# A two-layer diffusion transformer on one core: the background modulation units distributed anew over three stretches

## The chip, the cores and the metric

The kernel runs on one core of one Trainium2 chip. The metric is device time in microseconds from one launch, the median of three runs. A core has a tensor engine (PE; its weight loads are listed as PEld), a vector engine (DVE), a scalar engine (ACT), a general-purpose engine (POOL) and a sync engine (SP), which here only issues DMAs. Each engine works through its own queue in order and waits on semaphores for the others.

## The reference, cut to what matters

512 tokens of a sequence and 256 of a context, width 2048, go through two layers. Both layers modulate their normalised input and gate their output with vectors that come from one matrix each and two conditioning vectors (`c` for the sequence, `c_ctx` for the context):

```python
sc, scc = jax.nn.silu(c), jax.nn.silu(c_ctx)
for i in range(2):
    shift, scale, gate = jnp.split((sc @ ada_w[i] + ada_b[i])[:, None, :], 3, axis=-1)
    shift_c, scale_c, gate_c = jnp.split(scc @ ada_w[i] + ada_b[i], 3, axis=-1)
    h = rmsnorm(x, norm_w[i]) * (1.0 + scale) + shift
    hc = rmsnorm(xc, norm_w[i]) * (1.0 + scale_c) + shift_c
    y, yc = even_mix(h, hc, ...) if i == 0 else odd_mix(h, hc, ...)
    x = x + gate * y
    if i == 0:
        xc = xc + gate_c * yc
return rmsnorm(x, final_norm)
```

`even_mix` is an in-projection, a pooling branch, latent attention over 12 heads and an out-projection; `odd_mix` is an in-projection, a matrix memory (four heads, with gates), a window attention and an out-projection. In layer 1 the context only feeds keys, values and the initial state, so its gate is not needed.

## The kernel before, in words

All matrix products are done in three parts (high by high, high by low, low by high), so every weight block of [128, 512] is loaded by SP into `wraw` (3 buffers, `load_w`, L114), cast to its high part by ACT (L108, `wh`) and subtracted into its low part by DVE (L109, `wl`; 4 buffers each, that is two loads). `tmode` (L289 for the sequence's 512 columns, L291 for the context's 256) and `kmode` (L302) issue the products.

**The modulation** is a [2048, 6144] matrix by two vectors for each layer, cut into 24 units of 512 columns. Units 0 to 7 are layer 0's shift and scale, 8 to 11 its gate, 12 to 19 layer 1's shift and scale, 20 to 23 its gate. Units 0 to 7 are done on PE at the start. The others are background work (`Background`, `ada_vec_steps`), handed out in steps by calls of `bg.step(n)` between other work. A step takes one chunk of 128 rows: SP loads `at` (256 KB, L160, 4 buffers), DVE multiplies and adds it into `acc0` (L164), and where the context needs it too (units below 20) ACT multiplies `at` in place by the context's factor (L167) and POOL adds that into `acc1` (L169). After 16 chunks one step for each accumulator transposes and reduces it on DVE (L174, L175), and some steps into the next unit a tiny product (`pb`, L181) and four DVE additions (L131) finish the unit. So a unit has 18 steps, or 17 from unit 20 on, which touch neither ACT nor POOL.

**Stretch A, layer 0's in-projection.** `in_group(g)` does one group of 256 columns: four quarters, each with one `load_w`, a `bg.step(2)`, the products of four chunks with sequence and context, and another `bg.step(2)`, that is 16 steps for a group. There are twelve: two for the latent queries, four for the pooling branch (the second and fourth with `pool_mean` and `pool_mix` between their quarters: L512 to L528 on DVE, ACT and POOL, and the products `ppx` of L545 on PE), six for the attention's gates. Units 8 to 17 lie here: 180 steps in at most 192.

**Stretch B, layer 0's out-projection.** `out0(g, vs)` does a group of 256 columns in four quarters with a `bg.step(4)` in each: groups 1 to 5 with sequence and context, 6 and 7 with the sequence alone, then 0, 6 and 7 with the context alone, while `hx_chunks` prepares layer 1's rows on DVE, ACT and POOL. `out0_evac` (L855 to L864) evacuates a group with work on DVE, ACT and POOL. Units 18 to 23 lie here (18 and 19 with the context, 20 to 23 without): 104 steps in at most 160. `h_chunk` needs units 12 to 19; the gate of layer 1 is first read in the last out-projection.

**Stretch C, layer 1's in-projection**, has no background work before. In it `mv_group(h)` makes the values of heads 1 to 3 of the matrix memory (four quarters, `kmode`), after the gates of all heads were worked out in a long chain of small DVE and PE operations (pool `gs`, closed by `eg.close()`, its last reader among the buffers L1148). Then one group of keys and values of the window attention (weights `odw[5]`).

The order of instructions on PE is written out by hand only inside `manual_schedule`; elsewhere a scheduler orders each engine's queue, SP's too, by the order of the program and its own estimate of when an instruction's inputs and buffers are there. The pools of a stack reuse each other's space: a tile in a reused place waits until the earlier tile's last reader is done.

## Time and profile before

| | |
|---|---|
| median of three runs | 2376.73 us (2375.67 to 2378.95) |
| profiled execution, first to last instruction | 2376.1 us |
| PE busy | 2269.3 us (96%) |
| DVE busy | 1492.2 us (63%) |
| ACT busy | 1041.0 us (44%) |
| POOL busy | 462.4 us (19%) |
| mean granted clock of PE | 0.988 of 2.4 GHz |

The profile is of one execution. Times in its rows are microseconds from the span's start. A row of windows gives the busy time of each engine in a stretch, with the number of instructions that touch it, then the granted clock as a share of full speed. A row of a group gives line, engine, operation, what is written from what, the count, then busy time in us and mean ns of one, and after the last bar the engine's idle time just before and what ended it. A row of waits gives who waited for whom, total us, times and the longest.

### The profile page before, as it was taken

To read this page: it belongs to the slowest core of one execution; us is meant where nothing else is said; L and a number is where in the kernel's file an instruction comes from. 1 tells how busy PE (TensorE), PEld (TensorE's weight loads), DVE (VectorE), ACT (ScalarE), POOL (GpSimd) and SP (SyncE) were. 2 spreads that over 40 slices of the span, in tenths; PEclk is the share of its full clock that TensorE was granted. 3 is DMA by queue.
4 is the path that set the end of the run, shared out by engine and by line. 5 is a ranking of instruction groups with operands and counts; after the bars stand their busy time and mean duration, and the time that the engine had idled before them with its cause. 6 is when DMAs were issued, how large, how long until landed. Compare 5 with 4: busy or idle time off the path is not lost.

```text
span 2376.1 us, 34745 instructions
## 1 busy us (share of the span) xinstructions
PE 2269.3 (96%) x12920; PEld 1897.2 (80%) x12920; DVE 1492.2 (63%) x2748; ACT 1041.0 (44%) x2054; POOL 462.4 (19%) x393
## 2 busy tenths in 40 slices
PE   5999998899999999999999999999999999998997
PEld 3678887788888888878888798998888877776886
DVE  5578888866466666668767822522555576778435
ACT  4234444443344444454224522222555556666333
POOL 0015575754100000016311200000000000003111
PEclk9999999999999999999999999999999999999998
DMA  9854454553211111255675322123222211113333
GB/s 384 312 195 160 169 186 155 186 200 137 81 47 58 47 52 54 70 169 206 227 246 190 136 100 80 56 79 112 98 97 96 102 58 65 60 63 116 133 120 138
DMA packets 118586, 311.27 MB, mean 131 GB/s; under 512 B 13676, under 2 KB 21356, under 8 KB 118416
## 3 DMA queue, kind: packets, MB, share of 16 engines
q1 hardware_dynamic: 111536, 281.73, 34.5%
q0 software_dynamic: 6880, 27.32, 3.0%
q8 instruction: 101, 1.65, 0.3%
q14 instruction: 69, 0.57, 0.1%
HBM read 279.37 MB, written 29.62 MB: 130 GB/s over the span
## 4 chain that ended last, share of the span: by engine, by line
PE 70%; DVE 8%; issue 3%; ACT 2%; DMA 2%; POOL 2%; SPq 0%; DVEq 0%; ACTq 0%; POOLq 0%
PE px L289 20%; PE px L302 11%; PE pj L619 6%; PE pc L291 5%; PE px L1419 5%; PE s L683 5%; PE pc L302 3%; PE om L726 3%; PE pj L639 2%; PE s L1419 2%; PE po L1338 2%; PE tp L708 2%; POOL acc L169 1%; DVE wl L109 1%; DMA at<-in_ada_dram 1%
## 5 line engine op out<-in xcount | busy, mean ns | idle before, releaser
L109 DVE TENSOR_TENSOR wl<-wraw,wh 128x512 fp32r<-128x512 f32 (+2 forms) x556 | 429.9, 780 | 422.9 <-ACT wh L108 414.8
L108 ACT CAST wh<-wraw 128x512 fp32r<-128x512 f32 (+2 forms) x556 | 324.4, 589 | 605.8 <-PE pc L291 137.3
L169 POOL TENSOR_TENSOR acc<-acc,at 128x512 f32<-128x512 f32 x180 | 285.1, 1584 | 282.6 <-ACT at L167 272.5
L164 DVE SCALAR_TENSOR_TENSOR acc<-at,st,acc 128x512 f32<-128x512 f32 x240 | 246.5, 1027 | 53.5 <-DMA at<-in_ada_dram 49.6
L167 ACT ACTIVATE at<-at,st 128x512 f32<-128x512 f32 x180 | 130.0, 724 | 180.8 <-DVE acc L164 157.2
L302 PE MATMUL px<-wh,hxh 128*128 128x512 f32 (+2 forms) x512 | 174.2, 340 | 0.2 <-ACT akx L1201 0.2
L302 PE MATMUL px<-wl,hxh 128*128 128x512 f32 (+2 forms) x512 | 173.7, 339 | 0.0
L302 PE MATMUL px<-wh,hxl 128*128 128x512 f32 (+2 forms) x512 | 173.6, 339 | 0.0
L289 PE MATMUL px<-h0h,wl 128*128 128x512 f32 x384 | 155.6, 405 | 10.4 <-DVE wl L109 10.3
L289 PE MATMUL px<-h0h,wh 128*128 128x512 f32 x384 | 155.9, 406 | 1.3 <-ACT wh L108 1.3
L289 PE MATMUL px<-h0l,wh 128*128 128x512 f32 x384 | 154.1, 401 | 0.0
L291 PE MATMUL pc<-h0l,wh 128*128 128x256 f32 x400 | 113.8, 285 | 0.0
L291 PE MATMUL pc<-h0h,wh 128*128 128x256 f32 x400 | 113.7, 284 | 0.0
L291 PE MATMUL pc<-h0h,wl 128*128 128x256 f32 x400 | 113.7, 284 | 0.0
L302 PEld LDWEIGHTS px<-wh,hxh 128*128 128x128 f32 x512 | 96.2, 188 | 12.9 <-ACT sz L1262 1.0
L302 PEld LDWEIGHTS px<-wl,hxh 128*128 128x128 f32 x512 | 96.2, 188 | 11.3
L302 PEld LDWEIGHTS px<-wh,hxl 128*128 128x128 f32 x512 | 96.2, 188 | 11.0
L289 PEld LDWEIGHTS px<-h0h,wl 128*128 128x128 f32 x384 | 73.5, 191 | 31.1 <-DVE wl L109 13.9
L289 PE MATMUL px<-zxh,wh 128*128 128x512 f32 x224 | 89.6, 400 | 2.5 <-DVE x L855 2.5
L289 PE MATMUL px<-zxh,wl 128*128 128x512 f32 x224 | 89.2, 398 | 2.5 <-DVE wl L109 2.4
L289 PEld LDWEIGHTS px<-h0h,wh 128*128 128x128 f32 x384 | 73.6, 192 | 20.1 <-ACT wh L108 2.6
L289 PE MATMUL px<-zxl,wh 128*128 128x512 f32 x224 | 89.6, 400 | 0.0
(875 smaller groups left out, 6209.9 us busy)
## 6 DMA issues: line engine op xcount, KB each, us to landing
at<-in_ada_dram SPq DMA_DIRECT2D x256, 256.0 KB, 2.9
at<-in_ada_dram SPq DMA_DIRECT2D x64, 512.0 KB, 8.0
wraw<-in_od_in_dram SPq DMA_DIRECT2D x64, 512.0 KB, 3.4
wraw<-in_ev_in_dram SPq DMA_DIRECT2D x56, 512.0 KB, 4.2
wraw<-in_ev_out_dram SPq DMA_DIRECT2D x44, 512.0 KB, 4.2
wraw<-in_od_out_dram SPq DMA_DIRECT2D x36, 512.0 KB, 3.4
wraw<-in_od_oz_dram SPq DMA_DIRECT2D x32, 512.0 KB, 3.4
xt<-in_xT_dram SPq DMA_DIRECT2D x16, 384.0 KB, 7.5
```

The source lines that it names most:

```text
L108: S.copy(h, src)
L109: low.tensor_tensor(l, src, h, op=ALU.subtract)
L164: V.scalar_tensor_tensor(acc[0], at, st[:, kc, 0:1], acc[0], op0=ALU.mult, op1=ALU.add)
L167: S.mul(m, at, st[:, kc, 1:2])
L169: G.tensor_tensor(acc[1], acc[1], m, op=ALU.add)
L289: T.matmul(px[b], w_, Hx[kc][r_], start=s0, stop=s1)
L291: T.matmul(pc[b], w_, Hc[kc][r_], start=s0 and b == 0, stop=s1, skip_group_check=True)
L302: T.matmul(p_, h_, w_, start=s0, stop=s1, skip_group_check=True)
L619: T.matmul(t, w_, r_[:, sl], start=kc == 0 and n == 0, stop=kc == 3 and n == 2)
L683: T.matmul(s[:, c0 - k0 : c1 - k0], l_, r_[:, c0:c1], start=n == 0, stop=n == 4)
L726: T.matmul(o[:, :256], v_[:, 6 - nk + b, :], p_[:, b, :], start=b == 0 and n == 0, stop=b == nk - 1 and n == 2)
L1419: T.matmul(px[b], w_, Hs[kc][r_], start=first and i == 0 and n == 0, stop=last and i == len(kcs) - 1 and n == 2)
```

## The change

The units are handed out differently. Units 8 to 13 (108 steps) stay under the in-projection, with 16 steps for a group of the latent queries, 4 for the first group of each pooling pair and none for the second, 12 for the first four gate groups and 16 for the last two: 120 in all. Units 14 to 19 (108 steps) go under the out-projection with its 16 steps for a group, and are finished before the sequence's rows of layer 1 are begun, that is within groups 1 to 7 (112 steps). Units 20 to 23 (68 steps) go under layer 1's values, 20 steps for a group of `mv_group` (60) and 16 under the keys and values of the window attention, with buffers of their own (pool `ada1`, opened just after `gs` is closed). The instructions of a unit are the same as before. The diff also takes out comments and docstrings, which leaves every line at its number up to the insertions.

```diff
-    bg = Background(range(8, 18), pp, ap_, 4, "ta", 6)
-
-    def in_group(g, between=()):
+    bg = Background(range(8, 14), pp, ap_, 4, "ta", 6)
+
+    def in_group(g, between=(), steps=(1, 1)):
         px, pc = new_px(2), new_pc()
         for kq in range(4):
             w = load_w(win[g, kq])
-            bg.step(2)
+            bg.step(steps[0])
             tmode(px, [pc[:, b, :] for b in range(2)], w, range(4 * kq, 4 * kq + 4), HX0, HC0, kq == 0, kq == 3)
-            bg.step(2)
+            bg.step(steps[1])
             if kq < len(between):
                 between[kq]()
...
-        px, pc = in_group(2 + g)
+        px, pc = in_group(2 + g, steps=(2, 2))
...
-        px, pc = in_group(4 + 2 * pr)
+        px, pc = in_group(4 + 2 * pr, steps=(1, 0))
...
-        qx, qc = in_group(5 + 2 * pr, (lambda: mean(1), lambda: mix(0), lambda: None, lambda: mix(1)))
+        qx, qc = in_group(5 + 2 * pr, (lambda: mean(1), lambda: mix(0), lambda: None, lambda: mix(1)), (0, 0))
...
-        px, pc = in_group(8 + i)
+        px, pc = in_group(8 + i, steps=(2, 1) if i < 4 else (2, 2))
...
-    bg = Background(range(18, 24), pp, tz, 4, "ht", 3)
+    bg = Background(range(14, 20), pp, tz, 4, "ht", 3)
...
     for g in (6, 7):
         out0(g, (0,))
-    # layer 1's rows of the sequence, while the context goes through
+    bg.finish()
+
     ezx.close()
...
     for _ in hxs:
         pass
-    bg.finish()
     etz.close()
...
     eg.close()
 
-    # v of the other heads
+
+    ea = ExitStack()
+    bg = Background(range(20, 24), pp, opool(ea, "ada1"), 4, "atr", 1)
+
+
     def mv_group(h):
         px, pc = new_px(2), new_pc()
         pv = [px[b // 2][:, 256 * (b % 2) : 256 * (b % 2) + 256] for b in range(4)]
         for kq in range(4):
             w = load_w(odw[1 + h, kq])
+            bg.step(5)
...
         w = load_w(odw[5, kq])
+        bg.step(4)
         tmode(px, [pc[:, b, :] for b in range(2)], w, range(4 * kq, 4 * kq + 4), HX, HC, kq == 0, kq == 3)
+    bg.finish()
+    ea.close()
```

## Rows read from the trace of the kernel before

**Rows 1.** The page: busy time, share of the span and instructions of each engine.

```profile
PE 2269.3 (96%) x12920; PEld 1897.2 (80%) x12920; DVE 1492.2 (63%) x2748; ACT 1041.0 (44%) x2054; POOL 462.4 (19%) x393
```

**Rows 2.** Windows: latent queries, pooling, gate groups 1 and 2, 3 and 4, 5 and 6.

```profile
core 0: us, PE busy (x) PEld busy (x) DVE busy (x) ACT busy (x) POOL busy (x), PEclk, DMA share, GB/s
164.95:239.27 74.32, 71.54 (x400) 61.75 (x399) 66.25 (x72) 33.09 (x52) 43.10 (x30) 0.98 0.49 167
239.27:401.34 162.07, 149.41 (x812) 127.69 (x811) 140.26 (x161) 74.32 (x123) 94.35 (x70) 0.96 0.49 168
401.34:482.61 81.27, 73.70 (x391) 61.53 (x389) 69.76 (x70) 38.16 (x63) 61.34 (x42) 0.96 0.55 188
482.61:552.43 69.82, 68.97 (x390) 59.03 (x389) 38.15 (x47) 26.32 (x45) 28.42 (x21) 1.00 0.49 166
552.43:619.74 67.31, 67.31 (x389) 58.75 (x388) 38.41 (x52) 23.32 (x41) 25.90 (x19) 1.00 0.36 122
```

**Rows 3.** Waits: total us, times, longest; SP of 164:625, PE of 239:401 and 401:483.

```profile
SPq L160 <- POOL acc L169: 232.8, 143, 4.3
...
PE ppx L545 <- ACT wpoolh L108: 4.9, 2, 4.3
PE cps L247 <- DVE ssqc L454: 2.4, 1, 2.4
...
PE px L289 <- DVE wl L109: 6.3, 7, 1.9
```

**Rows 4.** The chain that ended last, gate groups 1 and 2, shares by line.

```profile
by line: issue 21.7%; DMA at<-in_ada_dram 19.4%; POOL acc L169 16.7%; DVE acc L164 14.1%; DVE wl L109 10.5%; ACT at L167 10.4%; DVE atr L174 3.0%; ACT wh L108 2.6%; DVE red L175 1.8%; DVE acc L162 0.7%; ACTq L167 0.3%; POOLq L169 0.1%; DVEq
```

**Rows 5.** Windows of the pooling stretch, lines L545, then L247 alone; columns PE, PEld.

```profile
239.27:401.34 162.07, 6.13 (x24) 4.58 (x24) 0.96 0.49 168
...
239.27:401.34 162.07, 1.50 (x12) 1.41 (x12) 0.96 0.49 168
```

**Rows 6.** Groups by line in 401:483, 1102:1136, 1204:1238 and 1238:1284.

```profile
L164 DVE SCALAR_TENSOR_TENSOR acc<-at,st,acc 128x512 f32<-128x512 f32 x37 | 41.7, 1127 | 8.7 <-DMA at<-in_ada_dram 8.1
L109 DVE TENSOR_TENSOR wl<-wraw,wh 128x512 fp32r<-128x512 f32 x15 | 22.4, 1498 | 4.1 <-ACT wh L108 4.0
...
L169 POOL TENSOR_TENSOR acc<-acc,at 128x512 f32<-128x512 f32 x12 | 19.6, 1635 | 6.3 <-ACT at L167 5.6
L164 DVE SCALAR_TENSOR_TENSOR acc<-at,st,acc 128x512 f32<-128x512 f32 x14 | 14.6, 1043 | 3.0 <-DMA at<-in_ada_dram 2.8
L174 DVE STREAM_TRANSPOSE atr<-acc 128x512 f32<-128x512 f32 x2 | 1.3, 686 | 0.0
...
L164 DVE SCALAR_TENSOR_TENSOR acc<-at,st,acc 128x512 f32<-128x512 f32 x15 | 11.6, 775 | 4.7 <-DMA at<-in_ada_dram 4.4
L109 DVE TENSOR_TENSOR wl<-wraw,wh 128x512 fp32r<-128x512 f32 x9 | 6.2, 686 | 1.4 <-ACT wh L108 1.4
...
L864 POOL TENSOR_TENSOR ssq<-ssq,sq 128x512 f32<-128x512 f32 x4 | 5.5, 1368 | 1.7 <-ACT sq L858 1.6
L855 DVE SCALAR_TENSOR_TENSOR x<-px,av,xr 128x512 f32<-128x512 f32 x4 | 3.0, 745 | 1.0 <-PE px L289 1.0
```

**Rows 7.** Windows: out-projection group 1, 2, 3 to 5, 6 and 7, context passes.

```profile
1060.53:1102.22 41.69, 36.69 (x194) 30.75 (x193) 36.35 (x37) 20.30 (x39) 27.52 (x21) 0.96 0.67 224
1102.22:1136.19 33.97, 33.97 (x196) 29.51 (x194) 25.23 (x28) 14.49 (x22) 22.73 (x18) 1.00 0.59 202
1136.19:1238.17 101.98, 101.98 (x582) 88.84 (x581) 69.37 (x109) 22.33 (x36) 22.27 (x22) 1.00 0.74 245
1238.17:1284.04 45.87, 45.87 (x201) 36.24 (x199) 31.15 (x54) 12.55 (x21) 9.28 (x10) 1.00 0.61 206
1284.04:1324.90 40.86, 37.98 (x305) 36.76 (x304) 36.34 (x63) 27.12 (x46) 13.28 (x10) 1.00 0.46 153
```

**Rows 8.** Windows: value products of heads 1, then 2 and 3; two timeline rows.

```profile
1480.08:1522.34 42.26, 42.26 (x361) 39.93 (x361) 30.95 (x119) 9.89 (x18) 0.67 (x3) 1.00 0.16 57
1522.34:1594.28 71.94, 71.69 (x603) 70.87 (x602) 17.91 (x33) 17.04 (x30) 1.20 (x4) 1.00 0.21 74
...
1512.12 0.19 DVE L1148 TENSOR_TENSOR mcol<-mcol,beta 128x32 f32<-128x32 f32 x1
...
1455.19 0.33 SPq L114 DMA_DIRECT2D wraw<-in_od_in_dram  x1
```

**Rows 9.** Waits of SP's queue, whole span.

```profile
SPq L160 <- PE s L683: 9.3, 1, 9.3
```

## The prediction

> **What bounds the kernel now.** I read the page's busy shares first: PE is busy for 96% of the span, no other engine for more than 63% [rows 1]. So PE's products set the length, and a change that leaves every product in place can only win back time in which PE stands or runs slowly. The question is where that time is and whether background work causes it. Second, I read the in-projection in windows [rows 2]. The last two gate groups take 67.31 us, 33.65 us each, with PE busy throughout at a granted clock of 1.00: the price of a group that nothing disturbs. Measured against it the stretch has this excess: the two latent-query groups 74.32 - 67.31 = 7.0 us, the four pooling groups 162.07 - 134.6 = 27.4, gate groups 1 and 2 81.27 - 67.31 = 14.0, groups 3 and 4 69.82 - 67.31 = 2.5; 50.9 us in all. Pooling and gates 1 and 2 are where DVE is busy for 86% of the time (140.26 of 162.07, 69.76 of 81.27) and where the granted clock falls to 0.96, so a stall is paid a second time by products at the lower of the two levels after it.
>
> Third, who ended the waits. In gates 1 and 2, PE waits 6.3 us for a weight's low part from DVE; in the pooling groups 4.9 us for a small weight that ACT casts and 2.4 us for a sum from DVE; SP waits 143 times, 232.8 us in all, with a background load until POOL has freed its buffer, and the next weights stand behind that load in SP's queue [rows 3]. Fourth, the chain that ended last in gates 1 and 2 hardly holds PE at all: it is the background's own circle, POOL's addition, the load into the freed buffer, DVE's addition, ACT's multiplication, with DVE's low parts caught in it [rows 4]. So in those groups the background work is the bound, and the projection waits for it.
>
> **The change, part by part.**
>
> *A, in-projection: four units fewer.* The query groups keep their 16 steps and their 7.0 us. The pooling groups go from 64 steps to 8. What remains of their 27.4 us is, first, work of PE: the 24 products of the pooling and 12 of the statistics have 6.13 and 1.50 us of busy time [rows 5], partly at the low clock, so I keep 6.5; second, the wait for the sum of the queries, of which I keep 2. That is 27.4 - 8.5 = 18.9 us won. Four gate groups go from 16 to 12 steps, without the lag that pooling handed on to them (groups 1 and 2 made 37 DVE additions in 81.27 us, two units' worth and more [rows 6]); I leave them 2 us of their 16.5 and win 14.5. The last two groups, untouched so far, get 16 steps; groups 3 and 4 show 2.5 us for a like load, so I charge 2. Part A: -18.9 - 14.5 + 2 = -31.4 us. Ends: -37.4 if all but PE's own 6 us goes from pooling, all 16 from the gates, and nothing comes back at the end. At the other end pooling's own chain keeps half of its stalls (-10), the gates keep 4 (-12), and the last two cost half of what gates 1 and 2 did (+7): -15. I take a value near the strong end because the chain of rows 4 names the background and not the pooling.
>
> The handover to the latent attention should not move: unit 13 ends with step 108, in the last group's second quarter, and unit 17 ended with step 180, in that same quarter. I charge nothing. If it moved, the attention's first loads would wait in the reused buffers.
>
> *B, out-projection: units with the context instead of units without.* Group 1 has such a unit today and takes 41.69 us, group 2 too, with 33.97 [rows 7]; both stay. Groups 3 to 5 take 101.98 us with mostly short units. Adding ACT's and POOL's part makes DVE's operations longer: its addition takes 0.775 us beside an idle POOL and 1.04 to 1.13 beside a busy one, its low part of a weight 0.686 and up to 1.498 [rows 6]. DVE's 69.37 us of 101.98 [rows 7] leaves room: +2 us, ends 0 and +6 (three groups at 2 us, near what gate groups 3 and 4 show).
>
> Groups 6 and 7 are the narrow place. They have no context products, so their 16 steps have 22.9 us each (45.87 for both [rows 7]) in place of 34. Steps 81 to 108 fall here: 24 chunks, four transposes and four reductions. On DVE: 24 x 1.127 = 27.0 us; 16 low parts of weights at 0.686 to 1.498 = 11.0 to 24.0; transposes at 0.686 and reductions counted alike 5.5; evacuation 4 x 0.745 = 3.0 [rows 6]. Sum 46.5 to 59.5 us for 45.87. On POOL: 24 x 1.635 = 39.2 and 4 x 1.368 = 5.5, together 44.7 [rows 6], which is all of the time, and POOL paces the loads in SP's queue as it does in stretch A. If DVE can be filled to 86% as in gates 1 and 2, the groups take 54 to 69 us: +8 to +23. Against that, engines run about a quarter ahead of PE. I take +12, ends 0 and +23. In the context passes behind, DVE is busy for 36.34 of 40.86 us [rows 7] with layer 1's rows; I charge nothing there, as the units end before, and name it below.
>
> *C, values of layer 1: four short units.* They add DVE work only: for each unit 16 x 0.775 us, a transpose of 0.686, a reduction as long, and four small additions, 14.4 us by estimate from rows 6; 57 us in all, of which 60 of 76 steps lie in the three value groups. DVE has 42.26 - 30.95 = 11.3 us free there with head 1 and 71.94 - 17.91 = 54.0 with heads 2 and 3, PE is busy all the time, and the DMA share is about 0.2 [rows 8]. The cover is there. What is dear is the gate chain, which runs until 1512.12 beside head 1's products [rows 8]: each of its small DVE operations can now stand behind an addition of 0.775 us while PE waits with the product that follows. I take +2, ends 0 and +10.
>
> *Sum.* -31.4 + 2 + 12 + 2 = -15.4 us. The profiled execution's span of 2376.1 us is 0.6 below the median of the runs, so I lay the sum on the median: 2376.7 - 15.4 = 2361 us. The ends added up give 2339 and 2401; they won't all fall together.
>
> **The rivals.**
>
> *1. The out-projection hands it back.* Groups 6 and 7 cost 23 us, groups 3 to 5 four, and part A comes out at -28: 2376.7 - 28 + 27 + 2 = 2378 at the worst, 2371 to 2380 as a case. For it: DVE's sum above its time, POOL at 97%. Against it: today's group 2, with the same load as groups 3 to 5 will have, shows 0.3 us of excess.
>
> *2. SP's queue stands before the values (slower).* `ada1` opens where `gs` was, so its loads wait until the gate chain's last reader at 1512.12. The weights of head 1's second quarter were loaded at 1455.19 [rows 8]. If the scheduler puts a background load ahead of them that must wait for that reader, they come 57 us later: load, cast and low part end near 1517, where PE needs them near 1480 + 42.26 / 4 = 1491. That is 26 us of PE standing and some 3 us at the low clock: 2361 - 2 + 29 = 2388 us. It happens already on a smaller scale: the first load of unit 18 waited 9.3 us on a reader in the attention (line 683) [rows 9]. It decides from the point where the wait is longer than the lead that three buffers give SP, some 20 us (three quarters of 71.94 / 8 = 9 us, less the load itself). Against it: the order of SP's queue comes from an estimate of when buffers are free, which would have to be wrong by that much.
>
> *3. The stalls are not the background's.* PE has the highest occupancy by far, the moved units lie beside its work before and after, and whatever stalls there are come from the projection's own casts and pooling; then the change moves hidden work: 2376 us, between 2372 and 2380. The Trainium skill (Perfetto Trace Analysis, Identifying the Most-Contended Engine) holds that the engine with the highest occupancy is the one to optimize first, which by the whole span speaks for this rival. The same section judges the tensor engine by its weight loads' busy share; here that is 80%, and both measures average over stretches in which, by rows 4, another circle is the bound. So the trace agrees for most of the span and not for gates 1 and 2.
>
> **How the numbers follow.** The forecast, 2342 to 2371, has a chance of 0.70; rival 1 0.14; rival 2 0.08; rival 3 0.08. About 0.2% (4.75 us) is what a measurement of this kernel can tell from no change, so faster means below 2372. The forecast gives 0.69 of faster and 0.01 of same; rival 1 spreads 0.04, 0.07, 0.03; rival 2 is slower; rival 3 is 0.01, 0.07, 0. Together faster 0.74, same 0.15, slower 0.11. The range, 2343 to 2377, leaves out rival 2, the worst of rivals 1 and 3, and a strip below: about 2 in 10.
>
> **What would show it right or wrong.** In the profile after: pooling groups near 143 us and gate groups 1 and 2 near 68, with a granted clock of 0.99 and more; the chain there made of PE again; the last two gate groups near 69. In the out-projection groups 6 and 7 near 58 us, with PE waiting for `wl` and SP for POOL. The context passes unchanged at 41 us. Head 1's values within 44 us, and no wait of SP for a reader of the gate chain that is longer than 15 us. I am wrong if pooling keeps more than 155 us (then its stalls are its own), if groups 6 and 7 take more than 66, or if the lag runs on into the context passes.

## The result: slower by 0.9%, and the profile after

The changed kernel takes 2396.07 us (2395.32 to 2401.75) against 2377.35 us (2375.67 to 2378.95) of the kernel before beside it: a ratio of 1.0086, 95% interval 1.0072 to 1.0100. The forecast was 2361 us, with a range of 2343 to 2377. The profiled execution of after has a span of 2395.0 us, 18.9 more than that of before. The page's busy shares, which answer to [rows 1], hardly move:

```profile
PE 2273.8 (95%) x12920; PEld 1903.5 (79%) x12920; DVE 1486.4 (62%) x2748; ACT 1042.3 (44%) x2054; POOL 458.4 (19%) x393
```

Where the time went, by windows over the same PE products in both traces (each row a difference of two windows, after less before):

| stretch | before | after | difference | predicted |
|---|---|---|---|---|
| start | 164.95 | 164.03 | -0.9 | 0 |
| latent queries | 74.32 | 73.78 | -0.5 | 0 |
| pooling | 162.07 | 145.84 | -16.2 | -18.9 |
| gate groups 1 to 4 | 151.09 | 135.77 | -15.3 | -14.5 |
| gate groups 5 and 6 | 67.31 | 67.59 | +0.3 | +2 |
| latent attention | 440.8 | 441.6 | +0.9 | 0 |
| out-projection, groups 1 and 2 | 75.66 | 74.55 | -1.1 | 0 |
| groups 3 to 5 | 101.98 | 122.19 | **+20.2** | +2 |
| groups 6 and 7 | 45.87 | 64.76 | **+18.9** | +12 |
| context passes | 40.86 | 41.07 | +0.2 | 0 |
| layer 1, up to head 1's values | 155.2 | 155.1 | 0 | 0 |
| values of heads 1 to 3, last keys and values | 150.1 | 161.5 | **+11.4** | +2 |
| rest | 745.9 | 747.2 | +1.3 | 0 |

Windows of after for latent queries, pooling, gate groups 1 and 2, 3 and 4, 5 and 6, which answer to [rows 2] (columns as there):

```profile
164.03:237.81 73.78, 71.02 (x399) 61.78 (x398) 65.84 (x72) 32.76 (x51) 42.71 (x30) 0.98 0.51 168
237.81:383.65 145.84, 143.39 (x809) 125.31 (x808) 77.13 (x97) 48.36 (x85) 36.45 (x33) 0.98 0.35 118
383.65:450.60 66.95, 66.95 (x389) 58.66 (x388) 34.57 (x40) 23.28 (x40) 24.59 (x18) 1.00 0.39 135
450.60:519.42 68.82, 67.48 (x390) 58.68 (x388) 35.08 (x42) 25.55 (x45) 26.56 (x20) 1.00 0.48 161
519.42:587.01 67.59, 67.59 (x392) 59.05 (x391) 41.81 (x54) 23.62 (x41) 25.75 (x19) 1.00 0.35 121
```

In gate groups 1 and 2 PE is now busy for the whole window at the full clock, and the chain that ended last there, in [rows 4] a circle of POOL, DMA, DVE and ACT, is PE's own:

```profile
by line: PE px L289 66.1%; PE pc L291 33.5%; PE ppx L545 0.4%; PE pb L181 0.3%
```

Windows of after for the out-projection, groups 1 to 7 one by one and then the context passes, which answer to [rows 7]:

```profile
1028.65:1069.66 41.01, 37.12 (x194) 31.38 (x193) 34.14 (x34) 19.07 (x36) 27.95 (x21) 0.92 0.71 240
1069.66:1103.20 33.54, 33.54 (x196) 29.15 (x194) 24.61 (x27) 14.25 (x21) 22.37 (x18) 1.00 0.55 185
1103.20:1141.01 37.81, 34.36 (x196) 29.55 (x194) 29.11 (x35) 16.66 (x25) 27.32 (x21) 0.98 0.61 200
1141.01:1183.09 42.08, 37.01 (x192) 31.30 (x192) 31.82 (x37) 17.36 (x26) 28.77 (x22) 0.94 0.53 182
1183.09:1225.39 42.30, 38.98 (x194) 32.81 (x195) 32.10 (x37) 16.55 (x25) 28.57 (x21) 0.88 0.53 176
1225.39:1254.08 28.69, 24.04 (x101) 17.61 (x99) 22.80 (x30) 13.09 (x21) 18.79 (x15) 1.00 0.55 192
1254.08:1290.15 36.07, 26.13 (x100) 19.05 (x101) 29.36 (x36) 14.02 (x24) 20.94 (x16) 0.95 0.55 179
1290.15:1331.22 41.07, 37.95 (x306) 36.75 (x305) 36.43 (x63) 27.14 (x46) 13.25 (x10) 1.00 0.47 153
```

Groups 3 to 5 had PE busy for all of their 101.98 us; now each lacks 3 to 5 us of it, and the clock goes down to 0.88. The chain of groups 3 to 7 is the circle that stretch A has lost:

```profile
by line: POOL acc L169 24.9%; DMA at<-in_ada_dram 15.7%; issue 13.0%; DVE acc L164 9.5%; DMA xr<-in_xT_dram 8.4%; DVE wl L109 6.5%; ACT at L167 5.8%; PE px L289 3.9%; DVE atr L174 2.6%; DVE x L855 2.2%; DMA wraw<-in_ev_out_dram 2.1%; DVE re
```

Waits of after in groups 3 to 7 (total us, times, longest), PE's and then those of SP's queue:

```profile
PE px L289 <- DVE wl L109: 14.4, 11, 2.8
...
PE px L289 <- ACT wh L108: 9.3, 4, 3.9
...
SPq L160 <- POOL acc L169: 86.8, 57, 3.6
SPq L114 <- DVE wl L109: 26.2, 13, 5.5
```

PE stands for a weight's low part (DVE) and for its high part (ACT). SP stands 57 times with a background load until POOL has freed the buffer. Groups by line of DVE and POOL in the same stretch, which answer to [rows 6]:

```profile
L164 DVE SCALAR_TENSOR_TENSOR acc<-at,st,acc 128x512 f32<-128x512 f32 x63 | 71.3, 1131 | 14.7 <-DMA at<-in_ada_dram 13.1 <-DVE wl L109 0.4
L109 DVE TENSOR_TENSOR wl<-wraw,wh 128x512 fp32r<-128x512 f32 x42 | 50.9, 1220 | 12.3 <-ACT wh L108 12.2
L855 DVE SCALAR_TENSOR_TENSOR x<-px,av,xr 128x512 f32<-128x512 f32 x11 | 8.2, 744 | 13.3 <-DMA xr<-in_xT_dram 12.3 <-PE px L289 1.0
...
L169 POOL TENSOR_TENSOR acc<-acc,at 128x512 f32<-128x512 f32 x64 | 99.9, 1560 | 36.1 <-ACT at L167 32.7
```

POOL makes 64 additions in the 186.95 us of these five groups, one in 2.92 us. By the starts in the trace, groups 3 to 5 hold 14, 15 and 14 of them and groups 6 and 7 hold 9 and 11.

In layer 1, windows of head 1, 2, 3 and the last keys and values, which answer to [rows 8]:

```profile
1486.36:1528.61 42.25, 42.25 (x360) 39.94 (x360) 33.86 (x124) 9.89 (x18) 0.67 (x3) 1.00 0.31 101
1528.61:1569.44 40.83, 37.79 (x304) 37.22 (x303) 32.43 (x55) 8.63 (x15) 0.67 (x3) 0.96 0.78 258
1569.44:1611.24 41.80, 37.52 (x305) 37.16 (x303) 31.62 (x53) 8.52 (x15) 0.53 (x1) 0.96 0.70 230
1611.24:1647.85 36.61, 36.46 (x211) 31.20 (x209) 10.28 (x25) 8.06 (x15) 0.09 (x1) 1.00 0.20 69
```

The units were given 20 steps for each head, but they lie almost wholly under heads 2 and 3, where 58 of their 64 chunks begin: DVE is busy there for 32.43 and 31.62 us (17.91 for both before), the DMA share is 0.78 and 0.70, and head 1 has nearly nothing of them. Waits in heads 2 and 3 and the last group, and one of SP's queue from head 1 on:

```profile
DVE acc L164 <- DMA at<-in_ada_dram: 17.2, 14, 2.4
...
ACT wvh L108 <- DVE wv L1185: 8.3, 3, 4.8
...
PE pc L1193 <- ACT wvh L108: 5.5, 2, 4.3
...
SPq L160 <- DVE negM L1141: 6.4, 1, 6.4
```

The last row is the late start: the loads wait in the reused space for the gate chain's readers, the second is issued at 1518.45, and from there the units run closely one behind the other. DVE stands 17.2 us for the loads; behind those additions in its queue stand the scaled values (`wv`, L1185), then ACT's high part of them, then PE's product.

### The profile page after: what moved, and what is told of

It reads as the page before. It is cut to its first block, busy times and chain, and to the rows that moved or that the text cites. A ratio compares the mean times of both kernels' runs of the same rounds, so it can differ in the third digit from the quotient of the medians.

```text
span 2395.0 us, 34724 instructions
## 1 busy us (share of the span) xinstructions
PE 2273.8 (95%) x12920; PEld 1903.5 (79%) x12920; DVE 1486.4 (62%) x2748; ACT 1042.3 (44%) x2054; POOL 458.4 (19%) x393
## 4 chain that ended last, share of the span: by engine, by line
PE 69%; DVE 8%; DMA 5%; issue 3%; POOL 3%; ACT 2%; SPq 0%; DVEq 0%; ACTq 0%; POOLq 0%
PE px L289 19%; PE px L302 10%; PE pc L291 6%; PE pj L619 6%; PE px L1427 5%; PE s L683 5%; DMA at<-in_ada_dram 3%; PE om L726 3%; POOL acc L169 3%; PE pc L302 2%; PE pj L639 2%; PE s L1427 2%; PE po L1346 2%; DVE acc L164 2%; PE tp L708 2%
## 5 line engine op out<-in xcount | busy, mean ns | idle before, releaser
L169 POOL TENSOR_TENSOR acc<-acc,at 128x512 f32<-128x512 f32 x180 | 280.4, 1558 | 279.8 <-ACT at L167 270.2
L289 PE MATMUL px<-zxh,wh 128*128 128x512 f32 x224 | 92.9, 415 | 11.4 <-ACT wh L108 10.9
L289 PE MATMUL px<-hxh,wh 128*128 128x512 f32 x224 | 89.7, 400 | 0.0
L289 PE MATMUL px<-hxl,wh 128*128 128x512 f32 x224 | 89.3, 399 | 0.0
```

The lines of the kernel that those rows point to most:

```text
L169: G.tensor_tensor(acc[1], acc[1], m, op=ALU.add)
L289: T.matmul(px[b], w_, Hx[kc][r_], start=s0, stop=s1)
```

## The experiments

All are edits of the changed kernel. "Groups 3 to 7" are those of the out-projection, 147.9 us in the kernel before and 186.95 in after; "the values" are heads 1 to 3 and the last keys and values, 150.1 and 161.5.

**Each part by itself.** `a_alone` has the changed kernel's in-projection, units 18 to 23 under the out-projection as in the kernel before, and nothing under the values. Units 14 to 17 are left out, and other units' vectors stand in for theirs.

```diff
-    bg = Background(range(14, 20), pp, tz, 4, "ht", 3)
+    for u in range(14, 18):
+        av[u] = av[u - 2]
+    bg = Background(range(18, 24), pp, tz, 4, "ht", 3)
...
-    bg = Background(range(20, 24), pp, opool(ea, "ada1"), 4, "atr", 1)
```

> The change's in-projection part alone: units 8 to 13 dealt as in the changed kernel, units 18 to 23 under the out-projection as before, nothing under the values of layer 1; units 14 to 17 are left out (their vectors are taken from units 12 to 15), so this is not the whole computation. If the in-projection's gain of 33.0 us (454.8 to 421.8 us in the two traces) stands by itself, the time is 2377 - 33 = 2344 us, with out-projection groups 1 to 7 at 224 us and heads 1 to 3 of the values at 114 us, as before. Rival: part of the gain is only moved, so that the attention behind the in-projection or the out-projection grows; then 2355 us or more.

2349.37 us (2347.78 to 2352.7), ratio 0.9885 [0.9868, 0.9901]; the in-projection as in after, groups 3 to 7 148.5, the values 150.2. Part A's gain stands without the other two parts, though 2344 us were expected. The profiled execution is 31.5 us faster in the in-projection and 25.2 in all; the other 6 us lie in pieces of at most 2.5 us over the other stretches, and what they are is open. The large losses of after, in groups 3 to 7 and under the values, are not there.

`no_c` leaves the units under the values out:

```diff
-    bg = Background(range(20, 24), pp, opool(ea, "ada1"), 4, "atr", 1)
...
-            bg.step(5)
```

> The changed kernel without the four units under layer 1's values (units 20 to 23 are left out, their vectors are taken from units 8 to 11). If these units alone cost what the stretch grew by (42.3 + 40.8 + 41.8 + 36.6 = 161.5 us against 150.1 before), the time falls by 11 to 13 us to about 2384 us and the stretch is back at 150 us. Rival: the out-projection's changes shift the schedule there too; then the stretch stays above 155 us.

2387.94 us in one run (2384 were expected; the profiled execution's last stretch is 3.3 us longer than that of after). The values are back at 150.2 (42.5, 36.0, 36.0 and 35.7), groups 3 to 7 keep 186. So the 11.4 us are those units', and the out-projection's loss doesn't depend on them.

**What of B is POOL's part.** `b_no_pool` does units 14 to 19 for the sequence only, without ACT's multiplication and POOL's addition:

```diff
-        both = u < 20
+        both = u < 14
...
```

> The changed kernel with units 14 to 19 computed for the sequence alone (ACT's multiplication, POOL's addition and the second transpose and reduction are left out, the context's vectors are copies). DVE's chunk additions and SP's 96 loads of 256 KB stay. Theory: the circle through ACT and POOL, and DVE's longer operations beside POOL, are what groups 3 to 7 wait for; then groups 3 to 5 fall from 122.2 to about 102 us and 6 and 7 from 64.8 to about 46, and the whole by some 39 us to 2357. Rival: DVE's additions and the loads in SP's queue are enough to stall the weights; then groups 3 to 7 keep more than half of the 39 us, and the whole stays above 2375.

2353.08 us; groups 3 to 7 take 151.7, and 3.8 of that is more in the last group alone. DVE's addition takes 760 ns and the low part 701, where after has 1131 and 1220. The background loads and DVE's additions into `acc0` are as many as in after (the second accumulator's transposes and reductions are gone too), so neither of these alone is what groups 3 to 7 wait for.

`b_pool_short` keeps the circle (load, DVE, ACT, POOL, buffer free) but POOL adds 64 of 512 columns:

```diff
+                    n_ = 64 if 14 <= u else 512
-                    G.tensor_tensor(acc[1], acc[1], m, op=ALU.add)
+                    G.tensor_tensor(acc[1][:, :n_], acc[1][:, :n_], m[:, :n_], op=ALU.add)
```

> The changed kernel with POOL's additions of units 14 to 19 on 64 of their 512 columns (the rest of the context's sums is left out); order of work, waits and buffers as they were. Theory 1 (POOL's time: it paces the loads and lengthens DVE's operations): groups 3 to 7 fall from 187.0 to about 153 us, as in the run without ACT and POOL (151.7), the whole to about 2360. Theory 2 (ACT's multiplication and the longer way around decide, not POOL's time): they stay above 175 us.

2351.75 us, groups 3 to 7 147.9. `b_pool_free` does the opposite: POOL works as long but on its accumulator alone, so that no buffer waits for it.

```diff
-                    G.tensor_tensor(acc[1], acc[1], m, op=ALU.add)
+                    G.tensor_tensor(acc[1], acc[1], acc[1] if 14 <= u else m, op=ALU.subtract if 14 <= u else ALU.add)
```

> The changed kernel with POOL's additions of units 14 to 19 taken off the circle: each runs on the accumulator alone, with 512 columns as before, and reads no load buffer, so a buffer is free after ACT (the context's sums are left out). POOL stays as busy beside DVE. If the circle through POOL (loads paced by its 1.6 us) is what costs, groups 3 to 7 fall to about 155 us. If DVE's longer operations beside a busy POOL are what costs (addition 1.13 us against 0.775, low part 1.22 against 0.69), they stay above 175 us.

2384.95 us, groups 3 to 7 170.8. Groups by line in groups 3 to 7 of `b_pool_free`:

```profile
L169 POOL TENSOR_TENSOR acc<-acc 128x512 f32<-128x512 f32 x60 | 80.7, 1345 | 5.3 <-ACT acc L167 0.9
L164 DVE SCALAR_TENSOR_TENSOR acc<-at,st,acc 128x512 f32<-128x512 f32 x61 | 77.5, 1271 | 2.7 <-DMA at<-in_ada_dram 1.4
...
L109 DVE TENSOR_TENSOR wl<-wraw,wh 128x512 fp32r<-128x512 f32 x42 | 41.0, 979 | 8.4 <-ACT wh L108 6.8 <-DMA at<-in_ada_dram 1.4
```

and of `b_pool_short`:

```profile
L164 DVE SCALAR_TENSOR_TENSOR acc<-at,st,acc 128x512 f32<-128x512 f32 x60 | 46.5, 774 | 18.1 <-DMA at<-in_ada_dram 16.9 <-DVE acc L164 0.2
...
L170 POOL TENSOR_TENSOR acc<-acc,at 128x64 f32<-128x64 f32 x60 | 29.1, 485 | 60.1 <-ACT at L167 59.7
L109 DVE TENSOR_TENSOR wl<-wraw,wh 128x512 fp32r<-128x512 f32 x40 | 28.6, 716 | 15.1 <-ACT wh L108 14.8
```

Of the 39 us, 16 go when POOL is off the circle (186.95 - 170.8), and the other 23 remain as long as POOL is busy beside DVE: there DVE's addition and low part are 0.5 and 0.26 us longer than in `b_pool_short`, though no load waits for POOL's addition any more. With a short POOL addition both are gone. The expectation had named 155 us for the one cause and more than 175 for the other; 170.8 lies between. The two shares hold for this order of taking things away: no run keeps the full circle while DVE is left alone, and in `b_pool_free` the first 15 of POOL's additions run ahead into the attention, which takes 447.7 us there for 441.6 in after. That all of the 23 us come through DVE's longer operations is argued from their size (61 additions and 42 low parts make 43 us more of DVE's time) and from PE's 10.6 us of waiting for low parts there; another 4.9 us of PE's waits are for high parts from ACT.

**Other waits of the stretch.** `b_ssq_dve` takes the sum of squares off POOL (in after SP also waits for it):

```diff
-                    (G if j < KC - 1 else V).tensor_tensor(ssq1[v], ssq1[v], sq[:, PARTS[v]], op=ALU.add)
+                    V.tensor_tensor(ssq1[v], ssq1[v], sq[:, PARTS[v]], op=ALU.add)
```

> The changed kernel with the sums of squares of the out-projection's evacuation on DVE in place of POOL (two operations for a block, some 0.7 and 0.4 us each). With POOL's additions off the circle, groups 3 to 7 kept 23 of their 39 us of excess. If most of that is the residual load that stands in SP's queue until POOL's sum of squares has freed a buffer, with the weights behind it, the groups fall from 187 to about 172 us. If it is DVE's longer operations beside a busy POOL, they stay at 183 us or more, for DVE then has more to do.

2385.96 us, groups 3 to 7 184.9: two of 39 us, where 15 were expected if that wait were the cause. `b_at5` gives the loads a fifth buffer:

```diff
-    bg = Background(range(14, 20), pp, tz, 4, "ht", 3)
+    bg = Background(range(14, 20), pp, tz, 5, "ht", 3)
```

> The changed kernel with five load buffers in place of four for units 14 to 19. If the circle's latency (buffer freed by POOL, load of some 3 us, DVE, ACT, POOL) is the limit, one buffer more shortens it by a fifth and groups 3 to 7 fall from 187 to about 175 us. If POOL's and DVE's throughput or the queue order is the limit, they stay within 4 us of 187.

2390.84 us, groups 3 to 7 182.2: 4.8 us less, where 12 were expected if the number of buffers were the limit. A buffer more lets SP run further ahead, but most of the loss stays. `b_atr_own` gives the transposed accumulator a buffer of its own instead of a place in the ring `ht`, which the out-projection's own tiles use too:

```diff
-    bg = Background(range(14, 20), pp, tz, 4, "ht", 3)
+    bg = Background(range(14, 20), pp, tz, 4, "atr", 1)
```

> The changed kernel with a buffer of its own for the transposed accumulators of units 14 to 19, so that the ring of three in the out-projection holds only the residual rows and their squares. In the trace of the changed kernel a residual load in SP's queue waits up to 6.9 us for a square's buffer (POOL's sum behind its additions), with the weights behind it. If the third user of the ring is what makes that wait, groups 3 to 5 fall from 122.2 to about 110 us and the whole by some 15 us to 2381. If the wait is for POOL's sum itself, they stay at 120 us or more.

2402.95 us in one run, a miss: it is no faster, and 1.2 us above the slowest of the four runs of after. Windows of `b_atr_own`, groups 2, 3, 4, 5 and then 6 and 7:

```profile
1071.36:1124.51 53.15, 42.60 (x196) 34.65 (x195) 44.39 (x41) 22.66 (x35) 42.07 (x31) 0.84 0.56 188
1124.51:1171.07 46.56, 38.67 (x196) 31.53 (x194) 37.71 (x40) 19.93 (x30) 33.85 (x26) 0.93 0.54 181
1171.07:1214.32 43.25, 36.60 (x193) 30.83 (x193) 36.00 (x39) 17.89 (x27) 28.91 (x22) 0.96 0.56 183
1214.32:1249.81 35.49, 34.66 (x197) 29.59 (x196) 25.86 (x33) 14.42 (x23) 22.13 (x18) 1.00 0.56 192
1249.81:1300.73 50.92, 47.95 (x200) 37.22 (x199) 27.03 (x44) 16.15 (x27) 18.42 (x16) 0.97 0.44 153
```

The loss moves forward with the units: group 2 has 31 operations of POOL instead of 18 (24 of its additions instead of 12) and is 20 us longer, groups 6 and 7 have 50.92 us instead of 64.76. Groups 1 to 7 take 270.2 us, where after has 261.5. The ring had spread the units out. How much of the 39 us its waits carry can't be read from this run; that they are not what makes the loss can.

**The additions moved.** `b_dve_both` lets DVE make both sums of units 14 to 19; ACT and POOL have no part in them.

```diff
-                S.mul(m, at, st[:, kc, 1:2])
-                if kc:
-                    G.tensor_tensor(acc[1], acc[1], m, op=ALU.add)
+                if u >= 14:
+                    if kc == 0:
+                        V.tensor_scalar(acc[1], at, st[:, kc, 1:2], None, op0=ALU.mult)
+                    else:
+                        V.scalar_tensor_tensor(acc[1], at, st[:, kc, 1:2], acc[1], op0=ALU.mult, op1=ALU.add)
+                else:
+                    S.mul(m, at, st[:, kc, 1:2])
+                    if kc:
+                        G.tensor_tensor(acc[1], acc[1], m, op=ALU.add)
```

> The changed kernel with both accumulations of units 14 to 19 on DVE, none on ACT and POOL: 96 more additions on DVE, each of the two at some 0.775 us with POOL idle, 1.55 us for a chunk in place of 1.13 beside POOL. By DVE's sum a group of sequence and context needs 14.2 x 1.55 + 8 x 0.69 + 5.5 of reductions and evacuations = 33 us of 34, so if only POOL's slowing and pacing matter, groups 3 to 7 fall from 187 to 165 or below. If DVE's own time is the bound in these groups, they stay above 180 us.

> The kernel of b_dve_both again, timed for an interval: 2354 as in its one look, ratio to the kernel before 0.990 to 0.992; groups 3 to 7 near 149 us.

2354.22 us in one run, and 2353.91 us (2349.08 to 2358.09) in four more, ratio 0.9895 [0.9870, 0.9920]. Windows of the second of these, groups 3 to 5, then 6 and 7:

```profile
1099.60:1202.22 102.62, 102.62 (x583) 88.15 (x582) 93.14 (x156) 19.42 (x31) 15.12 (x18) 1.00 0.66 221
1202.22:1248.66 46.44, 45.94 (x200) 36.21 (x199) 42.62 (x74) 12.67 (x21) 11.36 (x10) 1.00 0.63 210
```

and its groups by line for both sums, the low part and the evacuation there:

```profile
L171 DVE SCALAR_TENSOR_TENSOR acc<-at,st,acc 128x512 f32<-128x512 f32 x60 | 46.0, 767 | 0.0
L164 DVE SCALAR_TENSOR_TENSOR acc<-at,st,acc 128x512 f32<-128x512 f32 x60 | 45.2, 754 | 0.0
L109 DVE TENSOR_TENSOR wl<-wraw,wh 128x512 fp32r<-128x512 f32 x40 | 27.5, 701 | 6.2 <-ACT wh L108 6.0
L861 DVE SCALAR_TENSOR_TENSOR x<-px,av,xr 128x512 f32<-128x512 f32 x10 | 7.5, 751 | 5.3 <-DMA xr<-in_xT_dram 3.5 <-PE px L295 1.8
```

DVE is busy for 91 and 92% of the windows and PE loses half a microsecond. DVE makes the second sums in 46.0 us, and its other two groups give back as much: the first sums take 45.2 us (71.3 in after), the low parts 27.5 (50.9), 49.5 us less together. To hand the second sum to ACT and POOL saved DVE nothing.

**Where part C's 11 us come from.** `c_own_space` gives the units under the values buffers that no reader of the gate chain holds (idle parts of `aq0` and `az0`, and 4 KB more):

```diff
+    class Pick:
+        def tile(self, shape, dt, name, tag, bufs):
+            if tag == "acc0":
+                return aq0[0]
+            if tag == "atr":
+                return aq0[1]
+            self.n += 1
+            if self.n % 4 < 2:
+                return az0[:, self.n % 4, :]
+            return self.pool.tile(shape, dt, name=name, tag=tag, bufs=2)
...
+    bg = Background(range(20, 24), pp, Pick(opool(ea, "ada1")), 4, "atr", 1)
```

> The changed kernel with the buffers of units 20 to 23 in space that is idle then (the first window group's query and gate tiles, and 4 KB free beside them) in place of the space of the gate chain; still four buffers for the loads, the same steps at the same places. Theory: the units start late because their buffers wait for the gate chain's last readers (first load landed at 1515.9 us, second issued at 1518.5), and then 53 of 64 chunks are squeezed into heads 2 and 3; with own space the additions begin some 25 us earlier and heads 2 and 3 fall from 82.6 to about 74 us, the whole by 8 us to 2388. Rival: any 20 steps beside a value group stall DVE's other work through the loads' latency; then heads 1 to 3 together stay at 124 us.

2387.71 us. Heads 1 to 3 are back to what they were (42.3 and 72.5), but the units don't spread out: their additions run from 1372 to 1455, and head 0's values, 36.2 us in both kernels, take 42.3. Window of head 0:

```profile
1377.82:1420.12 42.30, 36.90 (x289) 36.23 (x287) 31.06 (x52) 7.56 (x18) 1.29 (x6) 1.00 0.86 278
```

The DMA share is 0.86 there, and PE has 5.4 us less than the window; the waits name 2.8 of them, for low parts of weights.

So 6.9 us (6.1 in head 0, 0.8 in the next group) move with the units; heads 1 to 3 and the last group take 151.4 where the kernel before has 150.1. Of the 11.4 us, about 8 are still there, and the late start has at most the other 3. `c_own_2buf` has the same with two load buffers, for a slower pace:

```diff
-            self.n += 1
-            if self.n % 4 < 2:
-                return az0[:, self.n % 4, :]
```

> As the run with buffers of their own for units 20 to 23, with two load buffers in place of four, so that the units run at half the pace (two chunks for each load's latency of some 4 us). In the run with four the cost moved to head 0's values (42.3 us in place of 36.2), where the units then ran. If it is the pace that costs (weights queued on SP behind a quick succession of loads, low parts behind additions that wait for them), head 0 is back at 36 to 37 us, heads 2 and 3 stay at 72.5, and the whole is about 2382. If any such unit costs some 1.5 us wherever it lies, the 6 us turn up in the key groups.

2397.64 us, a miss: head 0 costs 40.2, and the slower units now reach into the gate chain under head 1, which takes 51.2 instead of 42.3 (PE waits 6.8 us for the chain's `acol`, and the clock goes to 0.90). `c_gated` starts them between the two: one tiny DVE write of each buffer from the gates' tile holds the first loads back.

```diff
+            for i in range(2):
+                V.tensor_copy(az0[:, i, 0:1], GT[:, 0, 0:1])
+                V.tensor_copy(pool.tile([P, 512], F32, name=f"adag{i}", tag="ada", bufs=2)[:, 0:1], GT[:, 0, 0:1])
```

> The changed kernel with the gated buffers for units 20 to 23 alone; units 14 to 19 as changed. Theory 1: heads 1 to 3 and the last keys back to 150 to 153 us, 2385 to 2388 in all. Theory 2: those 11 us appear in head 0, in head 1 or in the keys before, 2393 to 2398.

`dve_gated` is this with the two sums on DVE:

> Units 14 to 19 with both accumulations on DVE, as in b_dve_both, and units 20 to 23 in buffers of their own (idle parts of aq0 and az0 and 4 KB more), each held back by one tiny DVE write from a tile of layer 1's gates, so that their loads start with head 0's values at the earliest and not in the gate chain's projections (1372) as in c_own_space. Theory 1 (part C's cost is the late start: units that begin at 1518 and are pressed into heads 2 and 3): heads 1 to 3 and the last keys cost 150 to 153 us as without the units, head 0 at most 37; with the 2354 of b_dve_both the time is 2343 to 2347. Theory 2 (the cost is the units' work itself on DVE and in SP's queue, wherever it lies under the values): it moves into head 0 and the gate chain, head 0 and 1 cost 5 to 12 us more, and the time is 2351 to 2358.

`c_gated` takes 2398.91 us in one run, and `dve_gated` 2356.4 us (2353.17 to 2357.12), ratio 0.9903 [0.9886, 0.9919]: nearest to the second theory in both. Heads 2 and 3 are free (72.6 and 72.8), head 0 is (36.2), and the cost is in head 1, 54.1 and 55.5 us for 42.3 (another 4 us and 1.4 lie in the group before it). Head 1's window in `dve_gated`, and then PE's wait from the view of waits:

```profile
1443.18:1498.67 55.49, 45.15 (x360) 42.17 (x360) 40.33 (x134) 9.90 (x18) 0.67 (x3) 0.88 0.30 100
```

```profile
PE pacr L1094 <- DVE acol L1088: 9.9, 1, 9.9
```

In `c_gated` the same wait is 9.5 us. Both kernels have additions of the units, which themselves wait for their loads, ahead of the chain's first small DVE operation, and PE stands for it, as the prediction had named it for the dear case of part C, with an end of +10. The mean granted clock of the window is 0.88.

`c_act_pool` asks whether it is DVE that must be spared: units 20 to 23 at their place, but with ACT multiplying and POOL adding (the rest as `b_dve_both`).

```diff
+            if u >= 20:
+                m = at if kc else acc[0]
+                S.mul(m, at, st[:, kc, 0:1])
+                if kc:
+                    G.tensor_tensor(acc[0], acc[0], m, op=ALU.add)
```

> As b_dve_both, and units 20 to 23 without DVE's 64 additions: ACT multiplies in place, POOL adds; place and buffers (4, where the gate chain's tiles were) as changed. Theory 2a (part C costs what it costs because DVE's additions stand in their queue for a load and the projection's values and low parts stand behind them): DVE is free again, heads 2 and 3 come back to 72 to 75 us and the time is 2341 to 2345. Theory 2b (what waits is whatever engine carries the background and the weights behind its loads in SP's queue): now ACT's multiplications stand for their loads and the casts behind them, or POOL's 64 additions of about 1.5 us make DVE's low parts longer; heads 2 and 3 keep 80 us and more, 2350 to 2360.

2371.48 us (2368.01 to 2374.13), ratio 0.9980 [0.9971, 0.9989], where `b_dve_both2` has 0.9895; heads 2, 3 and the last group take 135.7 us (119 with DVE, 108 without the units). Waits there:

```profile
DVE wl L109 <- ACT wh L108: 66.1, 19, 9.2
...
ACT at L163 <- DMA at<-in_ada_dram: 32.5, 30, 2.8
...
PE pc L1204 <- ACT wvh L108: 20.5, 4, 12.8
```

Now ACT stands 32.5 us for the loads with the casts behind it, and PE stands 20.5 us for ACT's high part of the values. DVE or ACT, the engine that carries the background stands for its loads, and what the projection needs from that engine stands behind. POOL's additions have a part in the cost too: DVE's low parts take 978 ns in this stretch, where they take 701 without a busy POOL in groups 3 to 7 of `b_dve_both2`. No run separates the two.

**Put together.** `dve_own` is `b_dve_both` with the buffers of `c_own_space`:

> As b_dve_both, and units 20 to 23 in the buffers of c_own_space, not held back. If the gains of the two add up: groups 3 to 7 near 149 us, head 0 near 42, heads 1 to 3 near 115, and 2348 to 2351, just under b_dve_both. If the units now run into DVE's work on layer 1's rows under the context passes (they end some 35 us earlier), the passes or the first keys take 5 us more and the time is 2353 to 2358.

2349.88 us (2347.96 to 2350.61), ratio 0.9890 [0.9874, 0.9907]: groups 3 to 7 148.5, head 0 43.2, the next group 36.1 instead of 33.6, heads 1 to 3 and the last group 151.5. It does all of the work and is 26 us faster than the kernel before beside it (2376.06 us), and so faster than both kernels. It can't be told apart from `b_dve_both2`, as the intervals overlap.

`redealt` tried a smaller load instead: units 8 to 15 under the in-projection with 16 steps for every gate group, 16 to 19 under the out-projection with 12, the last four as in `c_own_2buf`.

```diff
-    bg = Background(range(8, 14), pp, ap_, 4, "ta", 6)
+    bg = Background(range(8, 16), pp, ap_, 4, "ta", 6)
...
-            bg.step(4)
+            bg.step(3)
```

> A distribution by what the runs so far showed: units 8 to 15 under the in-projection (16 steps for a query or gate group, 8 for the first group of a pooling pair, none for the second), 16 to 19 under the out-projection with 12 steps for a group, 20 to 23 under layer 1's projection in their own space with two load buffers. If the gate groups hold 16 steps without loss (35.2 us at most in the changed kernel) and two units less take most of the out-projection's load away: in-projection 425 us, out-projection groups 1 to 7 at 230, the values as before, 2355 us in all. Rival: the scheduler draws the loads together as before and the out-projection's groups keep 20 us of excess; then 2370.

2374.27 us (2371.22 to 2375.58), ratio 0.9992 [0.9981, 1.0002], a miss. The last four gate groups take 144.57 us (136.4 in after), groups 1 to 7 229 (261.5 in after, 223.5 in before), and the values cost as in `c_own_2buf`. Fewer units beside POOL cost less, but not nothing.

## Why the prediction was wrong, point by point

- **What bounds the kernel, and part A: right.** -31.8 us over the windows of [rows 2] against -31.4. Pooling won 2.7 us less than said, gate groups 1 to 4 won 0.8 more and the last two cost 1.7 less, so the sum is nearer than its terms. The chain is PE's own again, as said, and `a_alone` shows the gain without the other parts. Rival 3 falls.
- **Part B, groups 3 to 5: the step that failed.** +2 us were predicted with an end of +6, and +20.2 came. For gate groups 1 and 2 the prediction had named the background's circle as the bound; here it priced the same circle by DVE's free time and by group 2 of the kernel before, with 0.3 us of excess. Group 2 can't carry that: it holds 12 additions of POOL [rows 6], groups 3 to 5 of after hold 14, 15 and 14. And group 1 does the same work with 8 us of excess, which the prediction left out of the price because that group keeps its unit. POOL's additions in group 1 and then in group 3 of the kernel before:

```profile
L169 POOL TENSOR_TENSOR acc<-acc,at 128x512 f32<-128x512 f32 x14 | 21.7, 1550 | 8.4 <-ACT at L167 7.7
...
L169 POOL TENSOR_TENSOR acc<-acc,at 128x512 f32<-128x512 f32 x4 | 6.6, 1659 | 1.7 <-ACT at L167 1.5
```

  Groups 1 and 2 together make 26 additions in 75.66 us [rows 7], one in 2.91 us, and leave some to group 3. The change puts 6 units x 15 = 90 of them into groups 1 to 7: by estimate 90 x 2.91 = 262 us, where these groups took 223.5 before. They took 261.5. That estimate would have shown the loss, but that it comes so near is partly luck: the pace is no constant (one in 2.70 to 3.28 us from group to group of after, and 24 additions in the 53.15 us of group 2 in `b_atr_own`, one in 2.2). What the runs show in place of the +2 is that the loss hangs on POOL's additions of full width: with 64 columns, or with both sums on DVE, groups 3 to 7 are at 147.9 and 149.1 us.
- **Groups 6 and 7: in the range, with the waits that were named.** +18.9 within 0 to +23, where +12 was taken. PE waits 10.0 us there for low parts, SP 22.6 us for POOL. The term was sized by 24 chunks; 20 of POOL's additions begin there, so groups 3 to 5 handed nothing on, and each of these takes 3.2 us of the stretch.
- **The price of a busy POOL: right in kind, too small in what it does.** The prediction had the longer DVE operations in [rows 6] (1.04 to 1.13 and up to 1.498 us) and concluded from DVE's free time (69.37 of 101.98) that they cost 2 us. DVE is busy for 29 to 32 us of 38 to 42 now, so it isn't full; what counts is the order. Each step goes through a load, DVE, ACT and POOL, and by `b_pool_free` and `b_pool_short` 16 of the 39 us go when POOL's addition leaves the circle and 23 stay as long as POOL is busy beside DVE.
- **Part C: +11.4, beyond its end of +10.** The cover was there, as said (DVE's time is free under the values). The gate chain that was feared went free in this kernel, head 1 took 42.25 us as before, since the loads came too late to meet it. The cost is in heads 2 and 3: 58 of the 64 loads and additions meant for 161 us are pressed into their 82.6, DVE stands for the loads and the values stand behind DVE. With other buffers the cost moves to head 0, or to the gate chain that the prediction had named; in no run did it vanish.
- **The rivals.** Rival 1 was right about the place and had 27 us at the worst, where 39 came. Rival 2 is there in a small form: the loads do wait for the gate chain's readers, 6.4 us in SP's queue, and PE doesn't stand for 26 us by it; and by `c_own_space` the late start has at most 3 us of part C's cost. The range stopped short of the worst of rival 1, and what came was beyond that worst.
- **What was to be seen.** Gate groups 1 and 2 near 68 (66.95), the last two near 69 (67.59), the context passes at 41 (41.07), head 1 within 44 (42.25), the wait of SP for the gate chain below 15 us (6.4): seen. Pooling near 143: 145.84, with a granted clock of 0.98 where 0.99 was said. Groups 6 and 7 near 58 with more than 66 as a sign of error: 64.76. Groups 3 to 5 weren't on the list at all.

What stays open: how the 23 us split between DVE's additions, its low parts and other waits behind a busy POOL, why the additions go at 2.2 us in one group and at 3.3 in another, and whether part C could go to nothing if the scheduler kept to the steps as written, one after each quarter; no run here had that.

## What to carry over

When background work goes round several engines, count from the trace how many of its steps a stretch has really done, not how many its lines call for; that rate, times the steps to be moved in, gives a first estimate of the new stretch, to be laid beside the estimate by busy time. An engine's free time is no cover for a step that waits for a load in that engine's queue, because what stands behind it waits too. And an addition handed to POOL to spare DVE can cost DVE more than the addition.

## What the runs showed of the hardware that was not expected

- Beside a busy POOL, DVE's operations with two inputs in on-chip memory get longer, the others looked at don't. In groups 3 to 7 of after against `b_dve_both2`: the addition 1131 against 754 ns, the low part 1220 against 701; but the evacuation, which takes one of its two inputs from PE's accumulators, 744 against 751. The trace also shows how. A pair of `b_pool_free`, POOL's row first:

```profile
1118.30 1.22 POOL L169 TENSOR_TENSOR acc<-acc 128x512 f32<-128x512 f32 x1
1118.66 1.41 DVE L164 SCALAR_TENSOR_TENSOR acc<-at,st,acc 128x512 f32<-128x512 f32 x1
```

  DVE's addition ends 0.55 us after POOL's. All 45 of DVE's additions that begin in groups 3 to 7 of that run while POOL still has more than 0.2 us of such an operation left end 0.54 to 0.55 us after it, whether 0.86 or 1.27 us were left (1.41 and 1.82 us long). In after it is 31 of 32 additions and all 22 low parts, 0.54 to 0.56 us after it. Additions that meet no operation of POOL take 0.75 us. So DVE stands until POOL's operation is over; it does not merely run at a slower rate. By the Trainium skill (SBUF — State Buffer, SBUF: two separate sides) DVE and GpSimd share a pair of ports under an exclusive lock, which a DVE operation with two inputs in SBUF needs against a GpSimd operation that reads SBUF, and the later of the two is blocked until the whole instruction of the other is over. The rows agree, in which operations are hit and in when they end.
- POOL's addition of 512 columns takes 1560 ns in after, 1345 on one input in `b_pool_free`; that of 64 columns takes 485 ns in `b_pool_short`, and beside it DVE's two operations are at 774 and 716 ns.
- Head 1 with a stall of PE of 9.9 us for one small operation takes 55.49 us in `dve_gated`, 13 more than in after: the mean granted clock of its window is 0.88, where the head without the stall has 1.00.
